# Rotary projection on one core: two of the last half-groups summed by accumulating transfers inside SBUF, and the last half in six units

## The chip, the cores and the metric

The kernel runs on one core of a Trainium2 chip. A core has TensorE (PE in the profile), VectorE (DVE), ScalarE (ACT), GpSimd (POOL) and SyncE (SP), a working memory of 128 partitions (SBUF), an accumulation memory of eight banks that only PE writes (PSUM), and 16 DMA engines shared by all queues. The metric is device microseconds of one execution. Three runs of the kernel before took 150.85, 151.02 and 152.38 us; the median is 151.02 us.

## The reference: what is computed

`x` is 16 x 512 x 768 in float32, `weight` is 768 x 768, `cos` and `sin` are 512 x 64, and there are 12 heads of 64 columns. The 512 rows of a batch share `cos` and `sin` with the other batches.

```
y    = matmul(x, weight)                 # 16 x 512 x 768
y1, y2 = halves of 32 columns of each head of y
out1 = y1 * cos1 - y2 * sin1
out2 = y2 * cos2 + y1 * sin2
out  = concatenate(out1, out2) per head  # float32, 16 x 512 x 768
```

## The kernel before, in words

**Tiles and groups.** A tile is 128 rows of one batch, every fourth row of its 512. Four tiles, of four batches and the same rows, make a group: 4 x 768 = 3072 output columns, which are exactly six PSUM banks of 512 float32 columns (`py`). There are 16 groups, 0 to 15 (`LAST`). A half-group is 1536 columns, that is two batches. All four batches of a group use the same 128 rows of `cos` and `sin`.

**Stages.** SP (and for some blocks POOL) loads `x`; ACT casts to fp16; PE transposes through the two banks `pt`, and ACT copies back to SBUF (some pairs of tiles are transposed on DVE instead). PE then multiplies by the weights, six chunks of the 768 inputs to each output piece. Groups 1 to 13 and a part of 14 are driven by a written-out order in which two row halves of PE run side by side (`both`, `walk`, `one`, L342 to L387). From tile 58, the third tile of group 14, the loop at L657 issues whole pieces in order (`mm_piece`, L330).

**Units.** `units(g)` (L301) cuts the columns of a group into stretches. When PE has finished a stretch, `rope(g, u)` (L394) is called for it. It issues a product on DVE (L412): the PSUM columns times two planes of `csn`, the cosines and the sines with sign, in one instruction that writes twice as many elements as the unit has columns. The products go to `tq`, to `w_raw` (the raw weights, no longer needed) or to an `xs` buffer. Then comes an add (L429): plane 0 plus plane 1 with the halves of each head swapped, into an output buffer `ov`. The add is POOL's for nearly all units. In the middle groups one add covers 1536 columns. In the tail the adds go unit by unit.

**The tail before.** Group 14 has units of 512, 1024, 512, 512 and 512 columns. Its first half has its products in `tq`, the second half in `w_raw`. The add of its last unit is put off and done by DVE after the product of the first unit of group 15 (`between`, L436 to L441). Group 15 has four units of 512 columns and four of 256, which use banks `ps4`, `ps5` and the two `pt` banks. POOL adds the first seven of them, and DVE adds the last one at the very end (`late`, L683).

**Orders and queues.** Every engine runs its instructions in program order, and `Flow.do` (L42) puts the semaphore waits in front of each. A store (L443, issued at L453) waits on its issuing engine for the adds that it reads. A wait there holds back everything behind it in the same queue. Groups 13 and 14 are stored by SP in halves of 768 KB, group 15 in pieces:

```
if s == 2:
    store(g, 0, H, "sp")
if s == 3:
    store(g, H, 2 * H, "act")
...
store(LAST, 2 * H, 2048, "sp")
store(LAST, 2048, 3 * H, "act")
store(LAST, 3 * H, 3 * H + 256, "sp")
store(LAST, 3 * H + 256, 3 * H + 512, "act")
for add in late:
    add()
store(LAST, 3 * H + 512, 4 * H, "sp")
```

`f.finish` (L686) makes SP wait for the landing of every store. Product buffers are taken in a ring: `HOMES` (L171) for half-groups, `HOMESL` for the units of group 15. Writes into `w_raw` are also guarded by the keys `W_HOME` (L161, L408), so one product there waits for the one before it.

Of the kernel before, what the change touches and what calls it, by code (L numbers as in the profile page):

```python
# [12 lines left out]
MULT = mybir.AluOpType.mult  # L13
# [3 lines left out]
class Flow:  # L17
# [24 lines left out]
    def do(self, e, make, reads=(), writes=(), dma=None, tick=True, after=0):  # L42
        need = {}
        for k in reads:
            for s, v in self.wrote.get(k, {}).items():
                need[s] = max(need.get(s, 0), v)
        for k in writes:
            for d in (self.wrote, self.readby):
                for s, v in d.get(k, {}).items():
                    need[s] = max(need.get(s, 0), v)  # L50
        if e == "pe":
            need.pop("pe", None)
            if after:
                need["pe"] = after
        waits = self.settle(e, need)
        for s, v in waits[:-1]:
            self.eng[e].wait_ge(self.sem(s), v)
        i = make(self.eng[e])
        if waits:
            s, v = waits[-1]  # L60
            i.wait_op(self.sem(s), v, "sem-ge")
        name, step = (dma, 16) if dma else (e, 1)
        self.sem(name)
        at = self.count[name] + step
        if tick or dma:
            i.then_inc(self.sems[name], step)
            self.count[name] = at
            self.known[name, at] = dict(self.seen[e])
        for k in reads:
            d = self.readby.setdefault(k, {})  # L70
            d[name] = max(d.get(name, 0), at)
        for k in writes:
            self.wrote[k] = {name: at}
            self.readby[k] = {}
        return i
# [30 lines left out]
def kernel(  # L106
# [11 lines left out]
    f = Flow(nc, tc)  # L118
# [49 lines left out]
        v = mem[:, base : base + 2 * n].rearrange("p (j n) -> p j n", j=2)  # L168
        return v[:, :, lo:hi], sorted(keys)

    HOMES0, HOMES, HOMESL = (0, 1024, 3072, 4096), (6144, 0, 3072), (0, 1024, 2048, 3072, 4096, 5120)  # L171
    ov_b = [sbuf(f"ov{i}", [P, QB * H], FP32) for i in range(NOV)]
    py = nc.alloc_psum_tensor("py", [P, 6 * 512], FP32).ap()
    pt2 = nc.alloc_psum_tensor("pt", [P, 2, 512], FP32).ap()
# [13 lines left out]
    def where(i):  # L188
        g, s = divmod(i, QB)
        return QB * (g // SB) + s, g % SB  # L190
# [110 lines left out]
    def units(g):  # L301
        if g < LAST:
            cut = [2560] if g == LAST - 1 else []
            at = [0, 512, 1536, 2048] + cut + [3072]
            return [(c, z, py[:, c:z], [f"ps{b}" for b in range(c // 512, z // 512)],
                     "dve" if (g, c) == (LAST - 1, 2560) else "pool")
                    for c, z in zip(at, at[1:])]
        u = [(c, c + 512, py[:, c : c + 512], [f"ps{c // 512}"], "pool")
             for c in range(0, 2048, 512)]
        if g == LAST:  # L310
            for k, (home, bank) in enumerate([
                (py[:, 2048:2304], "ps4"), (py[:, 2560:2816], "ps5"),
                (pt_b[0][:, 0:256], "pt0"), (pt_b[1][:, 0:256], "pt1"),
            ]):
                c = 2048 + 256 * k
                u.append((c, c + 256, home, [bank], "pool" if k < 3 else "dve"))
        return u

    def pieces(g, s):
# [69 lines left out]

    ov_of = {}  # L390

    late, between, tq_of = [], [], [0]

    def rope(g, u):  # L394
        c0, c1, ps, banks, adder = u
        w, r = c1 - c0, g % SB
        nh = w // D
        whole = 0 < g < LAST - 1 and (g, c0 // 1536) != (LAST - 2, 1)
        if adder == "dve" and g == LAST:
            k = len(late)  # L400
            tq, keys = xs_b[k][:, 0 : 2 * w].rearrange("p (j n) -> p j n", j=2), [f"xs{k}"]
        elif 0 < g < LAST:
            lo = c0 % 1536
            if lo == 0:
                tq_of[0] = HOMES[ring("tq", len(HOMES))]
            tq, keys = products(tq_of[0], 1536, lo, lo + w)
            if tq_of[0] >= 6144:
                keys = keys + W_HOME  # L408
        else:
            homes = HOMESL if g else HOMES0  # L410
            tq, keys = products(homes[ring(f"tq{g}", len(homes))], w, 0, w)
        do("dve", lambda eng: eng.tensor_tensor(  # L412
            out=tq.rearrange("p j (h d) -> p j h d", d=D),
            in0=ps.rearrange("p (h d) -> p h d", d=D)
            .unsqueeze(1).broadcast_to((P, 2, nh, D)),
            in1=csn[:, :, r, :].unsqueeze(2).broadcast_to((P, 2, nh, D)),
            op=MULT), reads=banks + ["csn"], writes=keys)
        if g not in ov_of:
            ov_of[g] = ring("ov", NOV)
        o = ov_of[g]  # L420

        if whole:
            if c0 % 1536 == 0:
                return
            c0, w = c0 - 512, 1536
            tq, keys = products(tq_of[0], 1536, 0, 1536)

        def add():
            do(adder, lambda eng: eng.tensor_tensor(  # L429
                out=ov_b[o][:, ds(c0, w)].rearrange("p (h t d) -> p h t d", t=2, d=HD),  # L430
                in0=tq[:, 0].rearrange("p (h t d) -> p h t d", t=2, d=HD),
                in1=tq[:, 1].rearrange("p (h t d) -> p h t d", t=2, d=HD)[:, :, ::-1, :],
                op=ADD), reads=[q for q in keys if q not in W_HOME], writes=[f"ov{o}c{c}" for c in range(c0, c1, 64)])

        if adder == "dve":
            (late if g == LAST else between).append(add)  # L436
        else:
            add()
        if g == LAST and c0 == 0:
            for more in between:  # L440
                more()  # L441

    def store(g, c0, c1, e):  # L443

        o = ov_of[g]
        b, r = where(g * QB)
        s0, s1 = c0 // H, -(-c1 // H)
        dst = out.rearrange("b (p r) h -> r p b h", r=SB)[r, :, b + s0 : b + s1]
        src = ov_b[o].rearrange("p (b h) -> p b h", b=QB)[:, s0:s1]
        if (c1 - c0) % H:  # L450
            dst = dst[:, 0, c0 - s0 * H : c1 - s0 * H]
            src = src[:, 0, c0 - s0 * H : c1 - s0 * H]
        do(e, lambda eng: eng.dma_start(out=dst, in_=src),  # L453
           reads=[f"ov{o}c{c}" for c in range(c0, c1, 64)], dma=f"ov{o}_{c0}")
# [151 lines left out]

    stores = {}
    for g in range(LAST):
        for h in (0, 2):
            i = QB * (g + 1) + h  # L610
            q = (g, h * H, (h + 2) * H, "act")
            if g < 3:
                i += g + 1
            elif g < LAST - 4:
                i += QB
            elif g < LAST - 2:
                i = QB * (LAST - 2) + 2 * (g - LAST + 4) + h // 2
            else:
                q = q[:3] + ("sp",)
            stores.setdefault(i, []).append(q)  # L620
# [21 lines left out]
    for i in range(QB, NTILE):  # L642
        g, s = divmod(i, QB)
        us = units(g)
        done_to = (s + 1) * H
        rows_on[0] = QB <= i <= QB * LAST
        if i < ROWS:
            if s % 2 == 0:
                for r in range(2):
                    lines[r].extend(walk(i // 2, r))  # L650
            for n in range(1, 4):
                both((i - QB) * 4608 + n * 1536)
                if n == (1 if i > QB else 2):
                    turns(i + T_AHEAD, 1)
        if i == ROWS:
            both(NTILE * 4608)
        for n, p in enumerate(pieces(g, s)) if i >= ROWS else ():  # L657
            a, z, _, bank = p
            if n == 1 and i < QB * LAST:
                turns(i + T_AHEAD, 1)  # L660
            for c in CHUNKS:
                mm_piece(i, p, c, c == CHUNKS[0], c == CHUNKS[-1],
                         tick=c == CHUNKS[-1])
            for u in us:
                if u[1] == z:
                    rope(g, u)
        bturns(i + B_AHEAD)
        turns(i + 1 + (T_AHEAD if i > QB else 2), 1)
        casts(i + 1 + (C_AHEAD if i > QB else 4), 1 + i % 2)
        pool_loads(i + P_AHEAD)  # L670
        for q in stores.get(i, ()):
            store(*q)
        if g == LAST:
            if s == 2:
                store(g, 0, H, "sp")
            if s == 3:
                store(g, H, 2 * H, "act")
    nc.gpsimd.drain()  # L678
    store(LAST, 2 * H, 2048, "sp")
    store(LAST, 2048, 3 * H, "act")  # L680
    store(LAST, 3 * H, 3 * H + 256, "sp")
    store(LAST, 3 * H + 256, 3 * H + 512, "act")
    for add in late:  # L683
        add()
    store(LAST, 3 * H + 512, 4 * H, "sp")
    f.finish("sp", [f"ov{o}c{c}" for o in range(NOV) for c in range(0, QB * H, 64)])  # L686


# [33 lines left out]
```

## Time and profile before

| what | value |
|---|---|
| median of three runs | 151.02 us |
| time of the profiled execution | 151.57 us |
| its span in the profile | 149.8 us |
| PE busy | 141.1 us (94%) |
| DVE busy | 126.4 us (84%) |
| POOL busy | 122.9 us (82%) |
| ACT busy | 78.0 us (52%) |
| moved by DMA | 51.27 MB, mean 342 GB/s |

The span is the stretch that the profiler records. The execution's time is 1.77 us longer. Busy shares are averages over the whole span: the first 20 us load the weights, the middle runs in a steady rhythm of PE, and the last 20 us are a tail with its own order. A chain is followed back from the last instruction; "issue" in it is time in which the profile shows nothing that was waited for. A landing time of a DMA runs from its issue to the arrival of its last byte.

### The profile page before, as it was taken

The numbers are of one execution on the slowest core, as the hardware profiler recorded it, in microseconds if no ns is written. First come the engines' busy times: TensorE is split into PE (matmuls) and PEld (weight loads), VectorE is DVE, ScalarE is ACT, GpSimd is POOL, SyncE is SP. The second block draws the span as 40 slices with busy tenths as digits, with TensorE's granted clock in tenths as the row PEclk, the third lists the DMA queues.
The fourth block names the chain that finished last, engine by engine and source line by source line (L and its number), as shares of the span: only waits on it lengthen the run. The fifth ranks groups of instructions, "written<-read, shape, count | busy, mean of one in ns | idle before, by whom it ended". The sixth has DMA issues, their size and how long they took to land.

```text
span 149.8 us, 4360 instructions
## 1 busy us (share of the span) xinstructions
PE 141.1 (94%) x1926; PEld 112.4 (75%) x1926; DVE 126.4 (84%) x92; ACT 78.0 (52%) x92; POOL 122.9 (82%) x68
## 2 busy tenths in 40 slices
PE   6969999999999999999999999999999999999940
PEld 2435578888888888888888888888888888856520
DVE  0154999887888899899999998999989998999980
ACT  3444798787777934456262905283336826163000
POOL 1000396999989998999999999999995979999990
PEclk9999999999999999999999999999999999999995
DMA  4999999999999999999999999999999999966683
GB/s 113 382 376 402 405 400 396 306 405 264 295 371 343 343 355 360 298 402 328 356 345 391 361 334 357 363 392 319 357 363 410 415 404 402 388 272 231 263 315 108
DMA packets 27555, 51.27 MB, mean 342 GB/s; under 512 B 7184, under 2 KB 13072, under 8 KB 27536
## 3 DMA queue, kind: packets, MB, share of 16 engines
q1 hardware_dynamic: 14592, 27.92, 53.9%
q10 hardware_dynamic: 7504, 21.10, 35.6%
q0 software_dynamic: 5440, 1.97, 10.7%
q8 instruction: 15, 0.25, 0.6%
q14 instruction: 4, 0.03, 0.1%
HBM read 27.79 MB, written 25.17 MB: 354 GB/s over the span
## 4 chain that ended last, share of the span: by engine, by line
PE 80%; DVE 6%; DMA 5%; POOL 3%; issue 2%; SPq 1%; POOLq 0%
PE py L360 70%; DMA w_raw<-in_weight_dram 5%; PE py L335 4%; PE pt L266 4%; POOL ov L429 3%; DVE w_raw L412 2%; DVE tq L412 2%; SPq L205 1%; PE pt L251 1%; DVE ov L429 1%; SPq L227 1%; POOLq L678 0%; DVE w_sb L185 0%; SPq L717 0%; SPq L116 0%
## 5 line engine op out<-in xcount | busy, mean ns | idle before, releaser
L429 POOL TENSOR_TENSOR ov<-tq 128x1536 f32<-128x1536 f32 (+3 forms) x31 | 77.5, 2520 | 19.4 <-DVE tq L412 19.3
L360 PE MATMUL py<-w_sb,xt 64*128 64x512 f16 (+1 forms) x864 | 81.4, 323 | 0.0
L412 DVE TENSOR_TENSOR tq<-py,csn 128x1024 f32<-128x1024 f32 (+2 forms) x46 | 74.6, 1652 | 5.2 <-PE py L360 4.9
L360 PEld LDWEIGHTS py<-w_sb,xt 64*128 64x128 f16 x864 | 61.0, 94 | 10.1 <-DVE tq L412 0.4
L185 ACT COPY xt<-pt 128x768 f16<-128x768 f16 x42 | 33.5, 800 | 45.7 <-PE pt L266 44.5
L185 ACT CAST xc<-xs 128x768 f16<-128x768 f32 x44 | 39.1, 907 | 13.9 <-DMA xs<-in_x_dram 13.7
L360 PE MATMUL py<-w_sb,xp 64*128 64x512 f16 (+1 forms) x432 | 42.6, 323 | 0.0
L412 DVE TENSOR_TENSOR w_raw<-py,csn 128x1024 f32<-128x1024 f32 (+1 forms) x21 | 35.2, 1674 | 3.7 <-PE py L360 3.5
L429 POOL TENSOR_TENSOR ov<-w_raw 128x1536 f32<-128x1536 f32 (+1 forms) x11 | 33.7, 3070 | 3.2 <-DVE w_raw L412 2.9
L360 PEld LDWEIGHTS py<-w_sb,xp 64*128 64x128 f16 x432 | 31.1, 94 | 4.7
L335 PE MATMUL py<-w_sb,xt 128*128 128x256 f16 (+1 forms) x90 | 15.7, 323 | 1.3 <-DVE w_sb L185 1.1
L266 PEld LDWEIGHTS pt<-ident,xc 64*128 64x128 f16 x456 | 14.8, 95 | 1.7 <-ACT xc L185 0.6
L266 PE MATMUL pt<-ident,xc 64*128 64x64 f16 x456 | 15.0, 190 | 0.0
L335 PEld LDWEIGHTS py<-w_sb,xt 128*128 128x128 f16 x90 | 8.1, 98 | 7.0 <-DVE w_sb L185 2.7
L220 POOL DMA_DIRECT2D xh<-in_x_dram x20 | 11.7, 590 | 0.0
L185 ACT CAST xd<-xb 128x1536 f16<-128x1536 f32 x5 | 8.2, 1636 | 0.2 <-DMA xb<-in_x_dram 0.2
L514 PE MATMUL py<-cold 128*128 128x512 f16 x12 | 5.0, 584 | 1.4 <-DVE cold L457 1.4
L185 DVE CAST w_sb<-w_raw 128x768 f16<-128x768 f32 x6 | 3.3, 558 | 3.4 <-DMA w_raw<-in_weight_dram 3.4
L294 DVE STREAM_TRANSPOSE xp<-xh 128x768 f32<-128x768 f32 x5 | 6.2, 1231 | 0.0
L185 DVE COPY xt<-pt 128x768 f16<-128x768 f16 x2 | 1.1, 558 | 5.5 <-PE pt L251 5.5
L294 DVE STREAM_TRANSPOSE xp<-xd 128x768 f32<-128x768 f32 x5 | 4.8, 969 | 0.0
L335 PE MATMUL py<-w_sb,xp 128*128 128x512 f16 (+1 forms) x24 | 4.2, 327 | 0.0
(20 smaller groups left out, 18.0 us busy)
## 6 DMA issues: line engine op xcount, KB each, us to landing
out_dram<-ov ACTq DMA_DIRECT2D x26, 768.0 KB, 8.6
xs<-in_x_dram SPq DMA_DIRECT2D x44, 384.0 KB, 17.7
xb<-in_x_dram SPq DMA_DIRECT2D x20, 192.0 KB, 17.4
out_dram<-ov SPq DMA_DIRECT2D x4, 768.0 KB, 4.7
w_raw<-in_weight_dram SPq DMA_DIRECT2D x6, 384.0 KB, 7.3
xh<-in_x_dram POOLq DMA_DIRECT2D x20, 96.0 KB, 12.9
out_dram<-ov SPq DMA_DIRECT2D x1, 384.0 KB, 2.6
out_dram<-ov ACTq DMA_DIRECT2D x1, 384.0 KB, 2.3
```

The source lines that it names most:

```text
L185: eng.copy(out=o, in_=i_) if e == "act" else eng.tensor_copy(out=o, in_=i_)
L205: do(e, lambda eng: eng.dma_start(out=xs_b[k], in_=x[b].rearrange("(p r) h -> r p h", r=SB)[r]), writes=[f"xs{k}"], dma=f"xs{k}")
L220: do(e, lambda eng: eng.dma_start(out=dst[ts(q, R)], in_=src[r, q]), writes=[f"{name}q{q}"], dma=name)
L227: do(e, lambda eng: eng.dma_start(out=w_raw[:, t, h], in_=wv[t, h]), writes=[f"wr{t}{h}"], dma=f"w{t}{h}")
L251: do("pe", lambda eng: eng.transpose(pt[:, t, h, :], src[:, t, h, :], ident), reads=[f"xc{c}", "ident"], writes=[f"pt{k}"], tick=(t, h) == ...
L266: do("pe", lambda eng: eng.transpose(pts[r][:, t, h, :], src[rows, t, h, :], ident[rows, rows]), reads=[f"xc{c}", "ident"], writes=[f"pt{r ...
L294: do("dve", lambda eng: eng.transpose(out=dst, in_=src), reads=rd, writes=[f"xp{z}"])
L335: do("pe", lambda eng: eng.matmul(ps, get(t, h), w_sb[:, t, h, a - s * H : z - s * H], start=start, stop=stop), reads=[key, f"w{t}{h}"], w ...
L360: do("pe", lambda eng: eng.matmul(py[:, a:z], get(t, h)[rows], w_sb[rows, t, h, a - s * H : z - s * H], start=start, stop=not opens and en ...
L412: do("dve", lambda eng: eng.tensor_tensor(out=tq.rearrange("p j (h d) -> p j h d", d=D), in0=ps.rearrange("p (h d) -> p h d", d=D) .unsque ...
L429: do(adder, lambda eng: eng.tensor_tensor(out=ov_b[o][:, ds(c0, w)].rearrange("p (h t d) -> p h t d", t=2, d=HD), in0=tq[:, 0].rearrange(" ...
L514: do("pe", lambda eng: eng.matmul(py[:, ts(b, 512)], cold[:, 0:P], cold, start=True, stop=warmed[0] < WARM - 6), reads=["cold"], writes=[f ...
```

## The change

The first 58 tiles are left as they are, up to the products of group 14's second half. Then:

- **Group 14, second half** (1536 columns, products in `w_raw`). Each of its three units gets two DVE products in place of one: plane 0 as before and plane 1 written with the halves of each head already swapped. When all six are done, POOL issues one DMA with `accum_op=ADD` that adds plane 1 onto plane 0 inside SBUF (128 partitions of 1536 float32, 768 KB). The two POOL adds and the DVE add of this half are gone. SP stores the sum from `w_raw`, in one DMA of 768 KB that waits for the accumulating DMA.
- **Group 15, first half.** The same, with three units of 512 columns, products in `tq`, an accumulating DMA of 768 KB, and one store of 768 KB issued by ACT. Its three POOL adds and its two stores of 384 KB are gone.
- **Group 15, second half.** Six units of 256 columns in place of one of 512 and four of 256, in banks `ps3`, `ps4`, `ps5`, `pt0`, `pt1` and `ps0`. POOL adds five and DVE the last. Each has one product instruction, and the products now lie in the upper half of `tq`.

```diff
-    HOMES0, HOMES, HOMESL = (0, 1024, 3072, 4096), (6144, 0, 3072), (0, 1024, 2048, 3072, 4096, 5120)
+    HOMES0, HOMES, HOMESL = (0, 1024, 3072, 4096), (6144, 0, 3072), tuple(range(3072, 6144, 512))
...
-                     "dve" if (g, c) == (LAST - 1, 2560) else "pool")
+                     "dma" if g == LAST - 1 and c >= 1536 else "pool")
...
-        u = [(c, c + 512, py[:, c : c + 512], [f"ps{c // 512}"], "pool")
-             for c in range(0, 2048, 512)]
...
+        u = [(c, c + 512, py[:, c : c + 512], [f"ps{c // 512}"], "dma")
+             for c in range(0, 2 * H, 512)]
+        for k, (home, bank) in enumerate([
+            (py[:, 1536:1792], "ps3"), (py[:, 2048:2304], "ps4"), (py[:, 2560:2816], "ps5"),
+            (pt_b[0][:, 0:256], "pt0"), (pt_b[1][:, 0:256], "pt1"), (py[:, 0:256], "ps0"),
+        ]):
+            c = 2 * H + 256 * k
+            u.append((c, c + 256, home, [bank], "pool" if k < 5 else "dve"))
...
+        if adder == "dma":
+            for j in range(2):
+                y = ps.rearrange("p (h t d) -> p h t d", t=2, d=HD)
+                m = csn[:, j, r, :].rearrange("p (t d) -> p t d", t=2)
+                if j:
+                    y, m = y[:, :, ::-1, :], m[:, ::-1, :]
+                do("dve", lambda eng: eng.tensor_tensor(
+                    out=tq[:, j].rearrange("p (h t d) -> p h t d", t=2, d=HD), in0=y,
+                    in1=m.unsqueeze(1).broadcast_to((P, nh, 2, HD)), op=MULT),
+                    reads=banks + ["csn"], writes=half(0 if g == LAST else tq_of[0], c0 % 1536 + 1536 * j, w))
...
+        if adder == "dma":
+            if c1 % 1536 == 0:
+                add_by_dma(g)
...
+    def add_by_dma(g):
+        v, keys = products(0 if g == LAST else tq_of[0], 1536, 0, 1536)
+        do("pool", lambda eng: eng.dma_start(out=v[:, 0], in_=v[:, 1], accum_op=ADD),
+           reads=keys, writes=[f"sum{g}"], dma=f"sum{g}")
+        sums[g] = v[:, 0]
+
+    def store_sum(g, e):
+        c0 = 0 if g == LAST else 2 * H
+        b, r = where(g * QB)
+        dst = out.rearrange("b (p r) h -> r p b h", r=SB)[r, :, b + c0 // H : b + c0 // H + 2]
+        do(e, lambda eng: eng.dma_start(out=dst, in_=sums[g].rearrange("p (b h) -> p b h", b=2)),
+           reads=[f"sum{g}"], dma=f"out{g}_{c0}")
...
-        if g == LAST:
-            if s == 2:
-                store(g, 0, H, "sp")
-            if s == 3:
-                store(g, H, 2 * H, "act")
     nc.gpsimd.drain()
+    store_sum(LAST - 1, "sp")
     store(LAST, 2 * H, 2048, "sp")
     store(LAST, 2048, 3 * H, "act")
+    store_sum(LAST, "act")
     store(LAST, 3 * H, 3 * H + 256, "sp")
     store(LAST, 3 * H + 256, 3 * H + 512, "act")
     for add in late:
```

The new helper `half` names the pieces of 256 columns of a product buffer that a plane's product writes; for `w_raw` it adds `W_HOME`, as before.

More of the change, by code (lines that the diff above doesn't have):

```diff
@@ L169, in products, with half @@
         return v[:, :, lo:hi], sorted(keys)
-    HOMES0, HOMES, HOMESL = (0, 1024, 3072, 4096), (6144, 0, 3072), (0, 1024, 2048, 3072, 4096, 5120)
+    def half(at, lo, n):
+        name, base = ("tq", at + lo) if at < 6144 else ("tw", at - 6144 + lo)
+        return [f"{name}{c // 256}" for c in range(base, base + n, 256)] + (W_HOME if at >= 6144 else [])
+    HOMES0, HOMES, HOMESL = (0, 1024, 3072, 4096), (6144, 0, 3072), tuple(range(3072, 6144, 512))
     ov_b = [sbuf(f"ov{i}", [P, QB * H], FP32) for i in range(NOV)]
@@ L305, in units @@
             return [(c, z, py[:, c:z], [f"ps{b}" for b in range(c // 512, z // 512)],
-                     "dve" if (g, c) == (LAST - 1, 2560) else "pool")
+                     "dma" if g == LAST - 1 and c >= 1536 else "pool")
                     for c, z in zip(at, at[1:])]
-        u = [(c, c + 512, py[:, c : c + 512], [f"ps{c // 512}"], "pool")
-             for c in range(0, 2048, 512)]
-        if g == LAST:
[L311 to L316, printed above, removed]
+        u = [(c, c + 512, py[:, c : c + 512], [f"ps{c // 512}"], "dma")
[6 more added lines that the diff above has]
+            u.append((c, c + 256, home, [bank], "pool" if k < 5 else "dve"))
         return u
@@ L390 @@
     ov_of = {}
-    late, between, tq_of = [], [], [0]
+    late, sums, tq_of = [], {}, [0]
     def rope(g, u):
@@ L398, in rope @@
         whole = 0 < g < LAST - 1 and (g, c0 // 1536) != (LAST - 2, 1)
-        if adder == "dve" and g == LAST:
-            k = len(late)
-            tq, keys = xs_b[k][:, 0 : 2 * w].rearrange("p (j n) -> p j n", j=2), [f"xs{k}"]
+        if g == LAST and adder == "dma":
+            tq, keys = products(0, 1536, c0, c1)
         elif 0 < g < LAST:
@@ L411, in rope @@
             tq, keys = products(homes[ring(f"tq{g}", len(homes))], w, 0, w)
[L412 to L417, printed above, removed]
+        if adder == "dma":
[8 more added lines that the diff above has]
+                    reads=banks + ["csn"], writes=half(0 if g == LAST else tq_of[0], c0 % 1536 + 1536 * j, w))
+        else:
+            do("dve", lambda eng: eng.tensor_tensor(
+                out=tq.rearrange("p j (h d) -> p j h d", d=D),
+                in0=ps.rearrange("p (h d) -> p h d", d=D)
+                .unsqueeze(1).broadcast_to((P, 2, nh, D)),
+                in1=csn[:, :, r, :].unsqueeze(2).broadcast_to((P, 2, nh, D)),
+                op=MULT), reads=banks + ["csn"], writes=keys)
         if g not in ov_of:
@@ L433, in add @@
                 op=ADD), reads=[q for q in keys if q not in W_HOME], writes=[f"ov{o}c{c}" for c in range(c0, c1, 64)])
-        if adder == "dve":
-            (late if g == LAST else between).append(add)
+        if adder == "dma":
+            if c1 % 1536 == 0:
+                add_by_dma(g)
+        elif adder == "dve":
+            late.append(add)
         else:
             add()
-        if g == LAST and c0 == 0:
-            for more in between:
-                more()
+    def add_by_dma(g):
[9 more added lines that the diff above has]
+           reads=[f"sum{g}"], dma=f"out{g}_{c0}")
     def store(g, c0, c1, e):
@@ L608 @@
     for g in range(LAST):
-        for h in (0, 2):
+        for h in (0, 2)[: 2 if g < LAST - 1 else 1]:
             i = QB * (g + 1) + h
@@ L672 @@
             store(*q)
-        if g == LAST:
-            if s == 2:
-                store(g, 0, H, "sp")
-            if s == 3:
-                store(g, H, 2 * H, "act")
     nc.gpsimd.drain()
+    store_sum(LAST - 1, "sp")
     store(LAST, 2 * H, 2048, "sp")
     store(LAST, 2048, 3 * H, "act")
+    store_sum(LAST, "act")
     store(LAST, 3 * H, 3 * H + 256, "sp")
@@ L685 @@
     store(LAST, 3 * H + 512, 4 * H, "sp")
-    f.finish("sp", [f"ov{o}c{c}" for o in range(NOV) for c in range(0, QB * H, 64)])
+    f.finish("sp", [f"ov{o}c{c}" for o in range(NOV) for c in range(0, QB * H, 64)]
+             + [f"sum{g}" for g in sums])
 _INS = ['x', 'weight', 'cos', 'sin', 'n_heads']
```

## The prediction

> **What bounds the kernel now.** I read the page first. PE is busy 94% of the span, but only until slice 38; the change lies behind tile 58, so what counts is the tail. I went to the busy table by stretches, then to the chain of waits at the end, the timeline of single engines, and the store issues. In the table the columns after the stretch are its length, busy time (and instructions) of PE, weight loads, DVE, ACT and POOL, the granted clock, the DMA share and GB/s:
>
> ```profile
> 136.00:138.00 2.00, 2.00 (x26) 1.23 (x24) 2.00 (x2) 0.46 (x2) 2.00 (x3) 1.00 0.50 195
> 138.00:140.00 2.00, 2.00 (x14) 1.13 (x12) 2.00 (x3) 0.70 (x1) 2.00 (x2) 1.00 0.55 203
> 140.00:142.00 2.00, 2.00 (x15) 1.32 (x14) 2.00 (x3) 0.00 (x0) 1.92 (x3) 1.00 0.99 386
> 142.00:144.00 2.00, 1.81 (x17) 1.37 (x14) 2.00 (x4) 0.00 (x0) 2.00 (x2) 1.00 0.69 269
> 144.00:146.00 2.00, 0.00 (x0) 0.00 (x0) 1.62 (x3) 0.00 (x0) 2.00 (x4) 1.00 0.86 325
> ```
>
> PE, DVE and POOL are all full from 136 to 142 us, so no engine has slack for the others. The DMA engines have some: a share of 0.50 and 0.55 at 136 to 140 us. The chain says who is last:
>
> ```profile
> 138.15 0.98 DVE ov L429
> 139.13 1.15 DVE tq L412
> ...
> 142.80 1.96 POOL ov L429 x2
> 144.76 0.68 POOLq L678
> 145.44 0.86 POOL ov L429
> ```
>
> The last add ends on POOL at 146.30 us. What follows is the last store of 128 KB, issued at 146.34 and landed 1.8 us later (148.14 us), and 1.66 us until the span ends at 149.8. DVE's own last add (145.02 + 0.70 = 145.72 us) is 0.6 us earlier.
>
> **The change, part by part.** All steps are placed on the profiled execution, span 149.8 us, own time 151.57 us; it lies 0.55 us above the median of 151.02 us. I work out how far the end of the span moves and add that to the median.
>
> ```profile
> 133.33 3.73 DVE L412 TENSOR_TENSOR w_raw<-py,csn 128x1024 f32<-128x1024 f32 x3
> 143.64 0.68 DVE L412 TENSOR_TENSOR tq<-pt,csn 128x512 f32<-128x512 f32 x1
> 144.24 0.68 DVE L412 TENSOR_TENSOR xs<-pt,csn 128x512 f32<-128x512 f32 x1
> 137.77 4.73 PE L335 MATMUL py<-w_sb,xt 128*128 128x256 f16 x30
> 142.33 1.47 PE L335 MATMUL pt<-w_sb,xt 128*128 128x256 f16 x12
> ```
>
> *DVE, group 14's second half.* Three products of 1024 elements become six of 512. Those into `w_raw` wait for one another: 1.22 us became a spacing of 1.25 (133.33, 134.58, 135.84). So a product of 512 there costs 0.675 + 0.03 = 0.70 us, six of them 4.2: they end at 137.55 us, 0.5 later than before. The swapped read from PSUM has no row. DVE's adds with swapped halves cost 0.705 us for 256 columns and 0.98 for 512, 1.07 ns per column. The products have the same slope (1.22 - 0.675 over 512). So I take nothing for it; at double the slope each swapped product would cost 0.55 more.
>
> *DVE, group 15's first half.* Six products without that wait, spaced 0.60 us as at 143.64 and 144.24. The DVE add of 0.98 us is gone, which pays for the delay. PE sets the pace now: from the two PE rows, 256 columns take (142.33 - 137.77) / 42 = 0.109 us. Columns up to 1536 are 6 + 12 such steps: 137.77 + 1.96, and 0.16 for the tail of the last matmul, gives 139.9 us. The last unit's two products then end at 139.95 + 0.60 + 0.675 = 141.2 us. No rearrangement on DVE or POOL can bring this forward.
>
> *DVE and POOL, last half.* Six products of 512 elements, 0.60 apart, from 141.2: the last ends at 144.8, DVE's late add at 145.6 (before 145.72). POOL loses five adds of 512 columns from the tail (two of group 14, three of group 15), and the unit 1536 to 2048 becomes two adds. Its five adds of 256 columns, spaced 0.68 us, start at 141.95 behind the DMA's issue and end at 145.4, 0.9 earlier than before. PE does the same columns, with twelve short matmuls for six long ones; at 0.109 us per 256 columns either way that is nothing.
>
> *The new chain.* The sum of group 15's first half must be issued by POOL, land, be waited for by ACT, and be stored. POOL is idle before both issues, so its waits (DVE at 137.55 and 141.2) hold back no add. The issue rows:
>
> ```profile
> out_dram<-ov SPq DMA_DIRECT2D x1, 768.0 KB, 3.5
> out_dram<-ov SPq DMA_DIRECT2D x1, 768.0 KB, 4.1
> L220 POOL DMA_DIRECT2D xh<-in_x_dram x20: 577/577/739, 29.7 to 97.8; - x20
> q10 hardware_dynamic: 7504, 21.10, 35.6%
> q0 software_dynamic: 5440, 1.97, 10.7%
> ```
>
> The first two are the least delayed stores of 768 KB (issued at 132.6 and 139.2 us), 3.8 us on average. ACT's store queue q10 has 21.10 MB in 0.356 x 149.8 x 16 = 853 engine-microseconds, 24.7 GB/s per engine, so 768 KB (49 KB per engine) keeps the engines for 2.0 us. What is left, 1.8 us, is fixed; 0.37 of it is the issue. On POOL an issue costs 0.58.
>
> An accumulating transfer is in no row of this trace. Its lower bound is a plain transfer: 0.58 + 1.4 + 2.0 = 4.0 us from the start of its issue to landing, a little less if a landing in SBUF is quicker than one in DRAM. Its upper bound goes by POOL's own queue, which casts: 1.97 MB in 0.107 x 149.8 x 16 = 256 engine-microseconds, 7.7 GB/s per engine, so 6.4 us of data. I take two plain passes, 4.0 us, since the engines must read both operands; that is nearer to the store rows, whose long rows are like these. To this comes half of group 14's store: its transfer lands at 137.6 + 0.6 + 1.4 + 4.0 = 143.6, SP stores it then, and its 2.0 us of data fall into the second transfer's. That is 1.0. So X, from POOL's issue to landing, is 0.58 + 1.4 + 4.0 + 1.0 = 7.0 us.
>
> Here the Trainium skill speaks more kindly. "DMA: Bandwidth & Descriptors", section "Anatomy of one DMA — SWDGE (gpsimd) path", fits any DMA issued from POOL as about 2.0 us plus its bytes at 436 GB/s: for 786,432 bytes an estimate of 3.8 us, near my lower bound. By it the sum would come to the second case below, about 152 us. The page does not say that the fit holds for accumulation, and no run here shows one.
>
> The last store by ACT costs 3.8 us. Behind it in ACT's queue stands the store of columns 2560 to 2816, whose add was long done: its 128 KB land 0.3 us after the large one. Then the 1.66 us as before. **The end of the span is 141.3 + X + 3.8 + 0.3 + 1.7 = 147.1 + X = 154.1 us**, 4.3 later than 149.8. From the median: 151.02 + 4.3 = **155.3 us**, slower by 2.8%. In terms of X the time is 148.3 + X.
>
> **The rivals.**
>
> *The transfers are hidden.* If X is below about 2.2 us, the end is DVE's late add again: SP's last store is issued at 145.7, lands 1.9 later (147.6), and the span ends at 149.3: 150.5 us. Not slower than before holds up to X = 2.7. For it: the DMA engines have room at 136 to 140 us. Against it: even a plain store of 384 KB, half the bytes, took 2.3 and 2.6 us. Note that the best this change can reach is 0.5 us (0.3%): PE, the last product and the last store stay.
>
> *It runs like a plain copy.* X of 4.0 to 5.5 us, with up to 1 us of collision: 152.3 to 153.8 us. For it: the engines may read both operands side by side, and the landing is in SBUF. Against it: three passages of the data instead of two. The fit named above belongs here.
>
> *It runs like POOL's cast queue.* Data 6.4 us each, X = 0.58 + 1.4 + 6.4 + 1.0 = 9.4, and if the second waits in the queue for the first (139.0 + 6.4 = 145.4 against 142.6), 12.2: 157.7 to 160.5 us. For it: it is the only queue that POOL writes. Against it: its packets are 362 bytes (1.97 MB / 5440); here rows are 6144 bytes.
>
> *The change doesn't do what it says* only if the sum of group 14 were the late one. It is issued 3.7 us earlier than the other, on the same queue, so no.
>
> **How the numbers follow.** Chances: two passes with collision (X 5.5 to 9.0, 153.8 to 157.3 us) 0.60; like a copy 0.16; like the cast queue or slower 0.19; hidden 0.05. One per cent (1.5 us) is about what a measurement of this kernel can tell from no change. It ends at 152.5 us, X = 4.2: only the hidden case and the quickest copies lie below. That makes 0.09 within 1%. Faster by over 1% would need an end that the PE and DVE rows exclude: 0.01. Slower 0.90. The range leaves out the hidden case and the upper end of the slowest: 152.3 to 160.0 us.
>
> **What would show it.** In the changed profile: products into `w_raw` spaced 0.70 us, the last of group 15's first half ending near 141.2; two DMA issues on POOL near 137.6 and 141.3; POOL's last add near 145.4; the accumulating transfers landing near 143.6 and 148.3; ACT's store of 768 KB issued right after the second; a chain that ends DVE, POOL's queue, DMA, ACT's queue, DMA, with DMA the only thing busy after 146 us. The sum is wrong if a transfer lands in under 4 or over 9 us, if the swapped products cost more than 0.70 us, or if POOL's issue takes long enough to hold back its adds.

## The result

The changed kernel takes 158.27 us (median of six runs, 158.1 to 161.63); the kernel before takes 151.12 us beside it. The ratio is 1.0471, 95% interval 1.0428 to 1.0515: slower by 4.7%. Forecast was 155.3 us in a range of 152.3 to 160.0 us. The direction held, and so did the price of the accumulating transfer; the loss was 7.15 us where 4.3 was worked out, since the last store cost more than its term. The profiled execution took 158.1 us with a span of 156.3 us.

Only the tail is changed. Since whole executions drift by one or two microseconds before the tail begins, I measure the **tail** from the start of the first product of group 14's second half (DVE into `w_raw`) to the end of the span. It is 149.8 - 133.33 = 16.5 us before and 156.3 - 133.65 = 22.65 us after, 6.2 us longer. The rest of the 7.15 us lies ahead of the tail (0.3) and in where the two profiled executions stand to their medians: before 0.45 us above, after 0.15 below.

### The profile page after: what moved, and what is told of

Read it like the earlier page. It is cut to its first block, busy times and chain, and to the rows that moved or that the text cites. A ratio compares the mean times of both kernels' runs of the same rounds, so it can differ in the third digit from the quotient of the medians.

```text
span 156.3 us, 4372 instructions
## 1 busy us (share of the span) xinstructions
PE 140.7 (90%) x1932; PEld 115.0 (74%) x1932; DVE 126.8 (81%) x98; ACT 78.0 (50%) x92; POOL 118.0 (75%) x66
## 4 chain that ended last, share of the span: by engine, by line
PE 81%; DVE 5%; DMA 4%; SPq 1%; issue 1%; DVEq 0%
PE py L363 67%; PE py L338 8%; PE pt L270 5%; DMA w_raw<-in_weight_dram 4%; DVE tq L425 2%; DVE tq L420 2%; DVE ov L442 1%; SPq L209 1%; PE pt L255 1%; SPq L231 1%; DVE w_sb L189 0%; SPq L741 0%; DVEq L57 0%; SPq L116 0%
## 5 line engine op out<-in xcount | busy, mean ns | idle before, releaser
L442 POOL TENSOR_TENSOR ov<-tq 128x1536 f32<-128x1536 f32 (+3 forms) x29 | 73.5, 2594 | 19.7 <-DVE tq L425 19.7
L425 DVE TENSOR_TENSOR tq<-py,csn 128x1024 f32<-128x1024 f32 (+2 forms) x44 | 71.3, 1650 | 5.2 <-PE py L363 5.0
L363 PEld LDWEIGHTS py<-w_sb,xt 64*128 64x128 f16 x864 | 62.6, 94 | 8.6 <-DVE tq L425 0.4
L363 PEld LDWEIGHTS py<-w_sb,xp 64*128 64x128 f16 x432 | 32.0, 94 | 3.9
L425 DVE TENSOR_TENSOR w_raw<-py,csn 128x1024 f32<-128x1024 f32 (+1 forms) x18 | 31.5, 1751 | 3.6 <-PE py L363 3.5
L442 POOL TENSOR_TENSOR ov<-w_raw 128x1536 f32<-128x1536 f32 x9 | 31.2, 3470 | 3.2 <-DVE w_raw L425 3.0
L270 PE MATMUL pt<-ident,xc 64*128 64x64 f16 x456 | 15.5, 190 | 0.0
L338 PEld LDWEIGHTS py<-w_sb,xt 128*128 128x128 f16 x96 | 8.6, 98 | 6.6 <-DVE w_sb L189 2.8
L420 DVE TENSOR_TENSOR w_raw<-py,csn 128x512 f32<-128x512 f32 x6 | 4.1, 689 | 0.2
## 6 DMA issues: line engine op xcount, KB each, us to landing
xs<-in_x_dram SPq DMA_DIRECT2D x44, 384.0 KB, 17.5
xb<-in_x_dram SPq DMA_DIRECT2D x20, 192.0 KB, 15.8
```

The source lines that it names most:

```text
L270: do("pe", lambda eng: eng.transpose(pts[r][:, t, h, :], src[rows, t, h, :], ident[rows, rows]), reads=[f"xc{c}", "ident"], writes=[f"pt{r ...
L338: do("pe", lambda eng: eng.matmul(ps, get(t, h), w_sb[:, t, h, a - s * H : z - s * H], start=start, stop=stop), reads=[key, f"w{t}{h}"], w ...
L363: do("pe", lambda eng: eng.matmul(py[:, a:z], get(t, h)[rows], w_sb[rows, t, h, a - s * H : z - s * H], start=start, stop=not opens and en ...
L420: do("dve", lambda eng: eng.tensor_tensor(out=tq[:, j].rearrange("p (h t d) -> p h t d", t=2, d=HD), in0=y, in1=m.unsqueeze(1).broadcast_t ...
L425: do("dve", lambda eng: eng.tensor_tensor(out=tq.rearrange("p j (h d) -> p j h d", d=D), in0=ps.rearrange("p (h d) -> p h d", d=D) .unsque ...
L442: do(adder, lambda eng: eng.tensor_tensor(out=ov_b[o][:, ds(c0, w)].rearrange("p (h t d) -> p h t d", t=2, d=HD), in0=tq[:, 0].rearrange(" ...
```

## The profile after

The timeline of the changed kernel (start, duration, engine, line, operation, tiles, count); L420 and L425 are products, L442 the adds, L458 the accumulating transfers, L466 the stores of their sums, L479 the other stores:

```profile
133.65 4.31 DVE L420 TENSOR_TENSOR w_raw<-py,csn 128x512 f32<-128x512 f32 x6
137.88 3.67 DVE L420 TENSOR_TENSOR tq<-py,csn 128x512 f32<-128x512 f32 x6
138.27 0.94 POOL L458 DMA_DIRECT2D w_raw<-w_raw  x1 [1.85 <-DVE w_raw L420]
141.85 0.87 POOL L458 DMA_DIRECT2D tq<-tq  x1 [2.64 <-DVE tq L420]
142.45 3.73 POOL L442 TENSOR_TENSOR ov<-tq 128x256 f32<-128x256 f32 x5
145.01 0.37 SPq L466 DMA_DIRECT2D out_dram<-w_raw  x1
145.24 1.24 DVE L442 TENSOR_TENSOR ov<-tq 128x256 f32<-128x256 f32 x1
148.68 0.38 ACTq L466 DMA_DIRECT2D out_dram<-tq  x1
149.10 1.24 ACTq L479 DMA_DIRECT2D out_dram<-ov  x1
```

The computing engines are done at 146.5 us, much as before (146.3). The last store is issued only at 149.10 us. The DMA issues (size, microseconds from issue to landing) say what lay between:

```profile
w_raw<-w_raw POOLq DMA_DIRECT2D x1, 768.0 KB, 6.7
tq<-tq POOLq DMA_DIRECT2D x1, 768.0 KB, 6.8
out_dram<-w_raw SPq DMA_DIRECT2D x1, 768.0 KB, 5.9
out_dram<-tq ACTq DMA_DIRECT2D x1, 768.0 KB, 5.3
```

The accumulating transfers land after 6.7 and 6.8 us. The stores of the sums need 5.9 and 5.3 us, where the two least delayed stores of this size took 3.5 and 4.1 us before. The table by stretches (last two columns: share of the 16 DMA engines, GB/s) shows why:

```profile
138.00:140.00 2.00, 2.00 (x24) 1.23 (x17) 2.00 (x4) 0.80 (x1) 0.94 (x1) 1.00 0.96 318
140.00:142.00 2.00, 2.00 (x19) 1.76 (x18) 2.00 (x4) 0.00 (x0) 0.15 (x1) 1.00 0.98 194
142.00:144.00 2.00, 2.00 (x20) 1.67 (x18) 2.00 (x5) 0.00 (x0) 2.00 (x4) 1.00 1.01 197
144.00:146.00 2.00, 0.14 (x2) 0.00 (x0) 1.90 (x3) 0.00 (x0) 2.00 (x4) 1.00 1.00 197
146.00:148.00 2.00, 0.00 (x0) 0.00 (x0) 0.48 (x1) 0.00 (x0) 0.18 (x1) 1.00 0.99 221
148.00:150.00 2.00, 0.00 (x0) 0.00 (x0) 0.00 (x0) 0.00 (x0) 0.00 (x0) 0.75 1.02 393
150.00:152.00 2.00, 0.00 (x0) 0.00 (x0) 0.00 (x0) 0.00 (x0) 0.00 (x0) 0.50 1.04 384
152.00:154.00 2.00, 0.00 (x0) 0.00 (x0) 0.00 (x0) 0.00 (x0) 0.00 (x0) 0.50 0.92 334
```

From 138 to 154 us the DMA engines have hardly a free moment (0.92 to 1.04). Before, they stood at 0.55 to 0.99 from 138 to 148 us and were idle then. For the stretches 142 to 144 and 148 to 150 us the queues are (packets, MB, share); q0 is POOL's queue, q1 SP's and q10 ACT's:

```profile
q0 software_dynamic: 79, 0.39, 100.6%
...
q1 hardware_dynamic: 262, 0.77, 99.8%
```

From 140 to 147.5 us POOL's queue q0 holds all engines and moves 0.197 MB per microsecond, so 786,432 bytes take 4.0 us. Group 14's store, issued at 145.01, has next to nothing moved before 148. Some 6 us of stores come behind the two sums.

## The experiments

Two theories after the result. **A, backlog:** each accumulating transfer takes all DMA engines for 4.0 us, other transfers wait meanwhile, and the end is the sum of the DMA work. **B, chain:** the end is the latency of the last accumulating transfer plus its store, whatever else is under way. The tail lengths of all runs, each from one profiled execution:

| kernel | span - start of tail | tail, us |
|---|---|---|
| before | 149.8 - 133.33 | 16.5 |
| no_sums | 148.7 - 132.91 | 15.8 |
| six_units | 149.8 - 133.24 | 16.6 |
| only14 | 153.7 - 134.91 | 18.8 |
| plain_copy | 153.1 - 133.30 | 19.8 |
| only15 | 153.0 - 132.83 | 20.2 |
| no_store14 | 154.9 - 133.95 | 20.95 |
| store14_last | 155.8 - 133.21 | 22.6 |
| changed kernel | 156.3 - 133.65 | 22.65 |
| after_again | 156.8 - 133.97 | 22.8 |
| early | 157.2 - 133.84 | 23.4 |

The changed kernel, its repetition and `store14_last` lie within 0.2 us of one another, and so do the kernel before and `six_units`; smaller differences than that are not read.

**no_store14.** The changed kernel without one store:

```diff
-    store_sum(LAST - 1, "sp")
```

> The changed kernel without the store of group 14's sum: this part of the output is left out, the two accumulating transfers and everything else stay. Theory A (backlog): from 139.5 to 154 us the DMA engines have no free moment, and the last store of 768 KB takes 5.3 us instead of 3.8 because 2.0 us of engine time of group 14's store lie in front of it. Then the time falls by 1.5 to 2 us, to 156.3-156.8. Theory B (chain): the end is set only by the last accumulating transfer (6.8 us) and the store that waits for it; group 14's store is not in that chain, and the time stays at 158.0-158.4.

Measured: 157.18 us, ratio 1.0327 (1.0237 to 1.0416); tail 20.95 us, 1.7 shorter. The two issue rows of the second half of the chain:

```profile
tq<-tq POOLq DMA_DIRECT2D x1, 768.0 KB, 7.0
out_dram<-tq ACTq DMA_DIRECT2D x1, 768.0 KB, 3.6
```

The accumulating transfer is as slow as in the changed kernel, and the store behind it lands in 3.6 us in place of 5.3. So 1.7 us of the loss is other work standing in front of the last store, which is A. The median missed A's bounds by 0.4 us, within its interval; beside it the kernel before stood at 151.69 us, and the loss against that is 5.5 us, again 1.7 less.

**store14_last.** The same store, moved behind all others in SP's order:

```diff
-    store_sum(LAST - 1, "sp")
...
     store(LAST, 3 * H + 512, 4 * H, "sp")
+    store_sum(LAST - 1, "sp")
```

> The changed kernel with the store of group 14's sum moved behind all other stores in SP's order; nothing else differs. Theory A (engines without a free moment from 139.5 us on): the same transfers in another order end at the same time, 157.8-158.6. Theory C (it is the store of group 14 ahead of group 15's that makes the last store late, and order matters): the store of group 15's sum lands in 3.8 us again, and the time falls by over 1 us, below 157.2.

Measured: 158.79 us, ratio 1.0454 (1.0358 to 1.055), beside 158.78 us of the changed kernel on the same chip (below); tail 22.6 us against 22.8 and 22.65. The small stores now go first, and the end stays. The order doesn't matter and theory C is out; what counts is the amount of work, as A says.

**after_again.** No edit.

> The changed kernel again, beside the next two on the same chip: 158.0-158.8.

158.78 us, ratio 1.0394 (1.0299 to 1.0489): the profile repeats (6.9 and 7.0 us for the accumulating transfers, 5.2 us for the last large store).

**only15.** Group 14 as in the kernel before:

```diff
-                     "dma" if g == LAST - 1 and c >= 1536 else "pool")
+                     "dve" if (g, c) == (LAST - 1, 2560) else "pool")
```

and with it the put-off DVE add and group 14's second store of before.

> Group 14's second half is added by POOL and DVE as in the kernel before; group 15's first half stays with its accumulating transfer, the last half in six units. Theory A: the transfer alone still takes 6.7 us from issue to landing (its own 4.0 us of engine time), but the backlog behind it is gone, so its store lands in 3.8-4.4 us; it is issued some 0.4 us later because DVE's add is back. Time 156.3-157.0. Theory B: the same chain, 0.4 us later: 158.4-158.8.

Measured: 154.94 us, ratio 1.0231 (1.0166 to 1.0296); tail 20.2 us, 3.7 more than before. B is out. A's bounds were 1.4 us too high, and the issue rows say why:

```profile
tq<-tq POOLq DMA_DIRECT2D x1, 768.0 KB, 5.8
out_dram<-tq ACTq DMA_DIRECT2D x1, 768.0 KB, 3.8
```

I had taken the 6.7 us of the first transfer for its time alone. Alone it is 5.8 us. In the changed kernel one of the 16 DMA engines is late by about a microsecond. The queues between 139.5 and 140 us, when the first transfer begins:

```profile
q0 software_dynamic: 15, 0.09, 92.4%
q8 instruction: 1, 0.02, 11.7%
```

Fifteen packets of q0 start, and one packet of q8, the queue that loads instructions, holds an engine for 0.117 x 16 x 0.5 = 0.9 us. Of the first transfer's 16 packets under 512 bytes, 15 come between 143.5 and 144 us and the last between 144.5 and 145; the transfer lands at 144.97. The second transfer has the first in front of it and ends in the same way: most of its small packets come before 148 us, the last one after. In `only15` the packet of q8 falls before 140 us and its transfer moves nothing before 142, so no engine is late. This is read from the traces; no run moved the load of instructions.

**only14.** Group 15's first half as in the kernel before:

```diff
-        u = [(c, c + 512, py[:, c : c + 512], [f"ps{c // 512}"], "dma")
+        u = [(c, c + 512, py[:, c : c + 512], [f"ps{c // 512}"], "pool")
```

and with it its two stores of 384 KB and product buffers of its own.

> Group 15's first half is added by POOL unit by unit and stored in two pieces as in the kernel before; group 14's second half stays with its accumulating transfer, the last half in six units. Theory A: the transfer holds all engines from 139.5 to 143.5 us, the two stores of 384 KB wait behind it, and 6 us of stores follow: last landing near 150.3, time 153-154.5. Theory B: its sum lands at 145.0, its store 3.8 us later, and the small stores behind it 0.3: end of the span near 150.8, time 152-152.6.

Measured: 154.05 us, ratio 1.0144 (1.0075 to 1.0213), inside A's bounds; tail 18.8 us, 2.3 more than before. The queues between 143 and 144 us, and the two stores of 384 KB issued at 143.0 and 144.25:

```profile
q0 software_dynamic: 39, 0.24, 120.2%
...
out_dram<-ov SPq DMA_DIRECT2D x1, 384.0 KB, 4.2
out_dram<-ov ACTq DMA_DIRECT2D x1, 384.0 KB, 3.8
```

These stores landed in 2.6 and 2.3 us before; now they wait until the accumulating transfer has let go. By the tails the parts nearly add up: 2.3 for group 14 and 3.7 for group 15 make 6.0 of 6.2 us. The medians say so less sharply: 2.4 and 3.25 us over the kernel before make 5.6 of 7.15, each with an interval of about 1 us to either side.

**six_units.** Both edits together, so no accumulating transfer at all, and only the cut of the last half is left.

> No accumulating transfer at all: groups 14 and 15 are added as in the kernel before, only the last half of group 15 is cut into six units of 256 columns instead of one of 512 and four of 256. Both theories: one add of 1.23 us on POOL becomes two of 0.68, DVE's products are the same, so 151.0-151.4, no change beyond 0.2%.

Measured: 152.09 us, ratio 1.0024 (0.9979 to 1.007); tail 16.6 us. The median lies above the expected bounds, but so does the kernel before beside it (151.69). The cut costs nothing that shows.

**no_sums.** The products are made, neither transfer nor its store is issued:

```diff
         if adder == "dma":
-            if c1 % 1536 == 0:
-                add_by_dma(g)
+            return
...
-    store_sum(LAST - 1, "sp")
...
-    store_sum(LAST, "act")
```

> The changed kernel without both accumulating transfers and without the two stores of their sums: the products are made, but group 14's second half and group 15's first half are left out of the output. It measures the floor of the change, were the transfers free. Both theories: POOL's and DVE's last adds and two stores of 128 KB are the end. By the prediction that is 0.5 us before the kernel before (150.4-150.8); if DVE's last add stays at the 1.24 us of the changed kernel's profile and is as late as there, it is no gain at all (151.0-151.4).

Measured: 151.06 us beside 151.74 us, ratio 0.9951 (0.9901 to 1.0001); tail 15.8 us, 0.7 less than before. The forecast's floor of 0.5 us holds within 0.2. In microseconds the median lies in the bounds of "no gain at all", but the kernel before stood higher here, and DVE's last add took 0.80 us, not 1.24. Since the two stores of 768 KB are left out as well, this is the most that the change could have reached. Even then the gain is smaller than what the measurement can tell from zero.

**plain_copy.** What does the accumulation itself cost?

```diff
-        do("pool", lambda eng: eng.dma_start(out=v[:, 0], in_=v[:, 1], accum_op=ADD),
+        do("pool", lambda eng: eng.dma_start(out=v[:, 0], in_=v[:, 1]),
```

> The changed kernel with both transfers inside SBUF as plain copies: POOL issues them in the same places, plane 1 replaces plane 0 and nothing is added, so the addition of these two half-groups is left out. If it is the accumulation that doubles the data time (theory A: two operands read, 4.0 us of all 16 engines against 2.0 for a store of the same size), each copy keeps the engines for 2.0 us, lands some 3.8 us after its issue in place of 6.8, and the time falls by 3.5 to 4.5 us, to 154-155. If a transfer from SBUF to SBUF on POOL's queue is as slow without the addition, the time stays at 158.0-158.4.

Measured: 155.15 us, ratio 1.0218 (1.015 to 1.0287); tail 19.8 us, 2.85 less than with accumulation. The issues, and the queue between 143 and 144 us:

```profile
w_raw<-w_raw POOLq DMA_DIRECT2D x1, 768.0 KB, 5.1
tq<-tq POOLq DMA_DIRECT2D x1, 768.0 KB, 3.6
...
q0 software_dynamic: 65, 0.40, 101.3%
```

A copy moves 0.40 MB per microsecond, the accumulation 0.197: it is the addition that doubles the data time, 2.0 to 4.0 us. The gain is less than the 3.5 to 4.5 us that I expected. The store of group 15's sum now starts earlier, at 145.1, but still lands in 5.4 us, since group 14's store and the small ones are in front of it. So more than half of the loss, 3.3 of 6.2 us, would remain with plain copies: it is the additional passage and the waiting for it.

**early.** Each unit's products are summed by a transfer of their own:

```diff
-            if c1 % 1536 == 0:
-                add_by_dma(g)
+            add_by_dma(g, c0 % 1536, c0 % 1536 + w)
```

> The changed kernel with each sum cut by unit: three accumulating transfers of 256 KB per half-group, each issued as soon as the products of its unit are there (rows of 2048 bytes in place of 6144); the stores are as before. Theory A: the engines' time for accumulation stays at 8 us in all and starts behind group 14's first store, so it ends at most 1 us earlier, and the same 6 us of stores follow: 157.0-157.8. Theory B: only the last transfer of 256 KB counts, landing some 3.5 us after its issue in place of 6.8: 154.5-155.5. If the engines serve stores between the shorter rows, group 14's sum is stored while group 15's is added, and DMA time is lost to neither.

Measured: 158.82 us, ratio 1.0422 (1.0322 to 1.0521); tail 23.4 us, 0.7 longer than the changed kernel; the medians don't separate the two. B would have shortened it by 3 us or more and falls. A's bounds were missed too, by 1.0 us: it expected a small gain. The queues between 142 and 143 us:

```profile
q0 software_dynamic: 109, 0.19, 114.6%
```

The transfers are issued from 136.55 us on, but their data begin only after 139.5 us, behind group 14's first store as before. With rows of 2048 bytes they move 0.18 to 0.19 MB per microsecond, so the two sums take 8.4 us in place of 8.0. Shorter rows let no store in between either: q1 has nothing between 142 and 148 us, although group 14's store is issued at 145.54.

## Why the prediction was right, and where its sum was short

- **What bounds the kernel, and the floor.** Right. PE's pace fixes when group 15's first half can be summed. The six products end at 137.88 + 3.67 = 141.55 us, 141.2 in the forecast; all of the difference is that this tail began 0.3 us later. `no_sums` shows the floor.
- **The products.** Right: 0.72 us each into `w_raw` (0.70 said), 0.61 into `tq` (0.60). The swapped read from PSUM costs nothing.
- **POOL's issue.** Small misses: 0.87 to 0.94 us instead of 0.58, and it begins 0.3 us after the last product ends, not 0.1. POOL's last add ends at 146.18 instead of 145.4, off the path.
- **X, issue to landing.** 6.8 us measured, 7.0 said, in part by luck. The data took 4.0 us as said (`plain_copy` shows that two passes is right). Alone it is 5.8 us (`only15`) against 0.58 + 1.4 + 4.0 = 6.0; what comes beside the data is right only as a sum, since the issue took 0.95 us, not 0.58. The collision of 1.0 has the right size and the wrong source: it was put down to group 14's store, and without that store X is still 7.0 (`no_store14`). In its place stand the first accumulating transfer and the late engine that `only15` brought out. The rule of the Trainium skill that was weighed ("DMA: Bandwidth & Descriptors", "Anatomy of one DMA — SWDGE (gpsimd) path", 2.0 us plus bytes at 436 GB/s) gives an estimate of 3.8 us: right for the plain copy that met a free queue (3.6), 2.0 us short for an accumulation (5.8).
- **The last store: the term that failed.** The forecast priced it as a store on free engines, 3.8 us, plus 0.3 for the small one behind it: 4.1. Measured from the second transfer's landing (148.65) to the last landing (149.10 + 5.4 = 154.5) it is 5.85 us. I had let group 14's store share the engines with the second accumulating transfer and be gone by then. In the trace it had to wait for that transfer's end, and so did the small stores; all of it then stood before the last store. `no_store14` (3.6 us again) and `store14_last` (no change) show this. The Trainium skill says in "DMA: Bandwidth & Descriptors", section "Queues, rings and completion order", that each DMA engine takes turns between the queues that have work for it. In the body of the changed kernel the trace agrees: between 68 and 69 us q0, q1 and q10 moved 69, 68 and 66 packets. In the tail, with q0 at 100%, SP's store issued at 145.01 us moved next to nothing before 148, and no turn is seen; for the tail the measurement decides.
- **The sum.** 154.1 + 0.3 (tail begins later) + 0.3 (POOL's issue) - 0.2 (X) + 1.75 (last store) + 0.1 (from last landing to the end) is 156.35 against a span of 156.3. The other 0.6 us of the median's miss is the distance of the two profiled executions from their medians (0.45 and 0.15).
- **The rivals.** "Hidden" and "like a plain copy" are out. The case that got 0.60, two passes with collision, has the right X but the wrong time: 158.27 us lies above its 153.8 to 157.3. The time lies in the bounds of "like POOL's cast queue" (157.7 to 160.5 us), but not for its reason: the data took 4.0 us, not 6.4. That the stated range holds the time is luck in this respect: its upper part was there for another mechanism.
- **What would show it.** The chain view didn't show the DMAs that were foretold: it follows SP's last store back to DVE's late add and ends at 146.5 us. The waits of SP's queue did: 5.0 us of waiting for landings at the very end.

## What to carry to other kernels

An accumulating transfer inside SBUF isn't a free adder. It keeps all DMA engines for twice the time of a store of the same bytes (4.0 us against 2.0 for 768 KB here), and the sum has yet to be stored. In a tail whose end is a store, price DMA work as a queue of engine time (every transfer issued before the last one, in full), not as a chain of latencies. And work out first what the change would gain if the moved work cost nothing: here 0.7 us, against 8 us of new engine time.

## What the runs showed of the hardware

- While an accumulating transfer moved its data, transfers on the hardware queues issued later moved next to nothing, with rows of 6144 and of 2048 bytes alike. This is no privilege of POOL's queue. In `early` POOL issued its first transfer at 136.55 us, and SP issued group 14's first store at 136.64; from 138 to 139 us that store moved alone (q1 at 103.1%) and q0 nothing. In the changed kernel ACT's store issued at 148.68 us moved next to nothing before 151 us, behind what SP had issued earlier (q1 at 100.3% from 150 to 150.75 us, then q10 at 95.0% from 151 to 152). So in the tail whole transfers followed one another, whichever queue they came from, while in the body, where loads of 384 KB landed after 17.5 us, the queues took turns by packets. What decides between the two was not tested.
- One packet of 16 KB that loaded instructions held one DMA engine for 0.9 us. The first accumulating transfers of five kernels, which began within 1.5 us of such a packet, landed after 6.6 to 6.9 us (changed kernel, `after_again`, `no_store14`, `store14_last`, `only14`); that of `only15`, which began over 2 us behind it, after 5.8.
- DVE's last add (two SBUF operands, 256 columns) took 1.22 to 1.32 us in the kernels in which an accumulating transfer ran beside it (changed kernel, `after_again`, `no_store14`, `store14_last`, `only15`, `early`), and 0.70 to 0.83 us where none was running (before, `six_units`, `no_sums`, `only14`); with the copies of `plain_copy`, just ended, it took 0.93. POOL's five adds of 256 columns took 3.73 us beside one and 3.46 us without one (`no_sums`) or beside a plain copy (`plain_copy`). Products from PSUM did not change. It was not on the path here, and its cause was not tested.
- An issue on SP or ACT while earlier transfers still waited took 1.24 us in place of 0.37 (ACT's last store at 149.10 us; SP's three small stores took 1.24 to 1.36).
- In the traces of these kernels only PE writes the PSUM tiles `py` and `pt`. The sentence at the start, that only PE writes PSUM, is shown in no other sense: no run here tries another engine.
